# Gate bias of a mixer trunk: seeded into the PSUM banks by ScalarE instead of added by matmuls

## The chip, the cores and the metric

The kernel runs on one core of a Trainium2 chip. The metric is the device time of one execution in microseconds (us). The engines are PE (TensorE), ACT (ScalarE), DVE (VectorE), POOL (GpSimd) and SP (SyncE, which here only issues DMAs).

## The reference

One decoder layer over 256 tokens of width 2048. Four token mixers (differential attention, mLSTM, gated linear attention "GLA", and S5) run on one projection of `h`. Each mixer's output is projected, multiplied by its own sigmoid gate, and summed; an output projection and a SwiGLU FFN follow.

```python
branches = (o_a, o_b, o_c, o_d)
merged = [jax.nn.sigmoid(h @ w_gate[l, i] + b_gate[l, i]) * (branches[i] @ w_branch[l, i])
          for i in range(N_BRANCH)]
mix = (merged[0] + merged[1] + merged[2] + merged[3]) @ w_out[l]
```

Only the term `+ b_gate[l, i]` is touched here: 4 branches times 2048 channels, the same for all 256 tokens.

## The kernel before, in words

Weights come from DRAM as 128x2048 f32 tiles (1 MB, tile `raw`, a ring of 3 buffers, loaded on SP's queue). ACT casts each half of a tile to a high part (`whi`, a CAST at L135), DVE subtracts to get the low part (`wlo`). A product is three matmuls per k step: `xh·wh`, `xh·wl`, `xl·wh` (`mm3t`), in rows `mmt<-whi,hx` and `mmt<-wlo,hx`.

The gate stage works through 16 groups (i, ng): branch i, 512 output channels ng. A group has four weight tiles (kq = 0 to 3), each giving 24 matmuls of 512 columns, 12 for each of two PSUM banks (`mmt`, one bank per 128 tokens, 4 buffers). When the fourth is done, ACT copies both banks into the SBUF tile `sig{i}{ng}` (`COPY sig<-mmt`), and later applies the sigmoid to it in place (`ACTIVATE sig<-sig`). The `sig` tiles come from a pool `f4` of 15 buffers. In order: the gates of branches 0 and 1, branch projections 0 and 1, gates 2, branch 2, gates 3, branch 3.

After each weight tile the mixers, written as generators, are advanced: three steps of a serial chain (attention, then mLSTM, then GLA) and a fraction of a step of S5. A mixer step goes back and forth: PE makes a product or a transpose into PSUM (`mxt`, `bu`, `ys`), ACT or DVE reads it, and PE needs the result again. The tile framework's scheduler then fixes the order in which each engine runs its instructions; each engine runs its own queue strictly in that order.

The bias of a group is added on PE. `gate_bias` prepares once a 128x256 tile `bhl` (high and low parts of all biases) and a selection tile `bsel`; at kq == 0 four matmuls `mmt<-bhl,bsel` of 256 columns open the two banks of the group, and the 96 weight matmuls add to them.

Of the kernel before, what the change touches and what calls it, by code (L numbers as in the profile page):

```python
# [11 lines left out]
F32R = mybir.dt.float32r  # L12
# [7 lines left out]
P = 128  # L20
# [47 lines left out]
def trunk(ctx: ExitStack, tc: tile.TileContext, A: dict, out: bass.AP):  # L68
# [101 lines left out]
    def f4t(name):  # L170
        return f4.tile([P, 4, 256], F32, name=name, tag="f4")
# [33 lines left out]
    for q in range(4):  # L205
        t = f4t(f"xT{q}")
# [78 lines left out]
        while len(hx) <= j:  # L285
            next(chunk_steps)


    bhl = mxc.tile([P, 256], F32R, name="bhl")
    bsel = mxc.tile([P, 32], F32R, name="bsel")  # L290

    def gate_bias():
        t = f4t("braw").rearrange("p a b -> p (a b)")
        ve.memset(t, 0.0)
        for q in range(4):
            sy.dma_start(t[32 * q : 32 * q + 16, 0:256], A["b_gate"][q // 2])
        sy.dma_start(t[:, 512:544], A["bsel"])
        se.copy(bsel, t[:, 512:544])
        se.copy(t[:, 256:512].bitcast(F32R), t[:, 0:256])
        for q in (0, 64):  # L300
            se.copy(bhl[q : q + 32, :], t[q : q + 32, 0:256])
            tt(bhl[q + 32 : q + 64, :], t[q + 32 : q + 64, 0:256], t[q + 32 : q + 64, 256:512], SUB)

    k0 = 0
    for r, kr in enumerate(ROUNDS):
        last = r == len(ROUNDS) - 1
        ahead = 0 if last else 3 * ROUNDS[r + 1]
        rest = GROUPS
        if r == 0:
            lead, rest = GROUPS[:NLEAD], GROUPS[NLEAD:]  # L310
            lb = {g: held[g] if g in held else [mmtile(), mmtile()] for g in lead}
            for ka in range(0, kr, 2):
                kb = min(ka + 2, kr)
                need(kb - 1)
                for g, gname in enumerate(lead):
                    get = weights(A["w_in0"][g][:, ka * 512 : kb * 512])
                    group_mm(lb[gname], get, [(k - ka, k) for k in range(ka, kb)], ka == 0, kb == kr)
            for gname in lead:
                if gname not in held:
                    group_out(gname, lb[gname], True)  # L320
        need(k0 + kr - 1)
        for i, gname in enumerate(rest):
            g = GROUPS.index(gname)
            gets = [weights(A[f"w_in{r}"][g][:, c : min(c + 2048, kr * 512)]) for c in range(0, kr * 512, 2048)]

            def get(off, width):
                return gets[off // 2048](off % 2048, width)

            keep = gname in held
            banks = held[gname] if keep else [mmtile(), mmtile()]  # L330
            group_mm(banks, get, [(k, k0 + k) for k in range(kr)], r == 0 or not keep, True)
            if not keep or last:
                group_out(gname, banks, r == 0 or keep)
            if last:
                take_ada(AW[i])
            for _ in range(ahead * (i + 1) // len(rest) - ahead * i // len(rest)):
                next(chunk_steps)
        get = weights(A[f"w_sm{r}"])
        bank = mmtile()
        for k in range(kr):  # L340
            mm2(bank, get(k * P, P), hx[k0 + k], k == 0, k == kr - 1)
        if r == 0:
            se.copy(small, bank[:, 0:256])
        else:
            tt(small, bank[:, 0:256], small, ADD)
        tt(small, bank[:, 256:512], small, ADD)
        if r == 1:
            gate_bias()
        k0 += kr


# [462 lines left out]
    def gate_unit(i, n):  # L814

        ng, kq = divmod(n, 4)
        get = weights(A["w_gate"][i, ng, kq])
        if kq == 0:
            gate_unit.banks = [mmtile(), mmtile()]
            for bank in gate_unit.banks:  # L820
                c = 4 * i + ng
                for q in range(2):
                    mm(bank[:, q * 256 : q * 256 + 256], bsel[:, q * 16 + c : q * 16 + c + 1].broadcast_to([P, P]),
                       bhl, q == 0, False)
        for tok, bank in enumerate(gate_unit.banks):
            for k in range(4):
                mm3t(bank, get(k * 512, 512), hx[4 * kq + k], tok, False, kq == 3 and k == 3)
        if kq == 3:
            t = f4t(f"sig{i}{ng}")
            sig[i, ng] = t  # L830
            for tok, bank in enumerate(gate_unit.banks):
                se.copy(by_token(t)[:, tok, :], bank)
        if n == NK - 1:
            for q in range(4):
                act(sig[i, q], sig[i, q], AF.Sigmoid)
# [251 lines left out]
def layout(i):  # L1087
# [41 lines left out]
    for r, kr in enumerate(ROUNDS):  # L1129
# [4 lines left out]
        k0 += kr  # L1134
    a["w_gate"] = c_(np.asarray(i["w_gate"], f)[0].reshape(4, 4, 4, P, 4, 512).transpose(0, 4, 1, 3, 2, 5)
                     .reshape(4, 4, 4, P, D))
    a["b_gate"] = c_(np.asarray(i["b_gate"], f).reshape(16, 2, 256).transpose(1, 0, 2))
    bs = np.zeros((P, 32), f)
    bs[:16, :16] = bs[32:48, :16] = bs[64:80, 16:] = bs[96:112, 16:] = np.eye(16, dtype=f)
    a["bsel"] = bs  # L1140
    a["w_branch"] = c_(np.asarray(i["w_branch"], f)[0].reshape(4, 4, P, 4, 512).transpose(0, 3, 2, 1, 4)
                       .reshape(4, 4, P, D))
    a["w_out"] = c_(np.asarray(i["w_out"], f)[0].reshape(4, 4, P, 4, 512).transpose(3, 0, 2, 1, 4)
# [64 lines left out]
```

## Time and profile before

| | us |
|---|---|
| median of 3 runs | 1692.04 (1691.89 to 1694.96) |
| the profiled execution | 1693.66 |
| its span in the trace | 1691.9 |
| PE busy | 1652.8 |
| DVE busy | 1242.0 |
| ACT busy | 874.8 |

The span is what the trace covers of the profiled execution; the remaining 1.8 us lie around it. PE's mean granted clock was 0.993 of full speed. Gate and branch stages lie between about 280 and 840 us.

### The profile page before, as it was taken

The numbers are of one execution on the slowest core, as the hardware profiler recorded it, in microseconds if no ns is written. First come the engines' busy times: TensorE is split into PE (matmuls) and PEld (weight loads), VectorE is DVE, ScalarE is ACT, GpSimd is POOL, SyncE is SP. The second block draws the span as 40 slices with busy tenths as digits, with TensorE's granted clock in tenths as the row PEclk, the third lists the DMA queues.
The fourth block names the chain that finished last, engine by engine and source line by source line (L and its number), as shares of the span: only waits on it lengthen the run. The fifth ranks groups of instructions, "written<-read, shape, count | busy, mean of one in ns | idle before, by whom it ended". The sixth has DMA issues, their size and how long they took to land.

```text
span 1691.9 us, 20679 instructions
## 1 busy us (share of the span) xinstructions
PE 1652.8 (98%) x8000; PEld 1349.1 (80%) x8000; DVE 1242.0 (73%) x1721; ACT 874.8 (52%) x1270; POOL 0.2 (0%) x4
## 2 busy tenths in 40 slices
PE   6999999999999999999999899999999999999997
PEld 4788888777787777777888688888888888888886
DVE  6889999898899998997657766666666555444444
ACT  4544445687675465465445744444444444444342
POOL 0000000000000000000000000000000000000000
PEclk8999999999999999999999899999999999999999
DMA  9887886865556765765566266666665555555553
GB/s 370 358 339 306 317 353 256 298 253 211 195 214 251 294 251 187 263 252 191 207 239 258 100 224 225 245 228 245 227 244 203 192 182 190 211 197 199 189 187 121
DMA packets 61134, 400.69 MB, mean 237 GB/s; under 512 B 6881, under 2 KB 10470, under 8 KB 13676
## 3 DMA queue, kind: packets, MB, share of 16 engines
q1 hardware_dynamic: 60460, 398.33, 63.7%
q8 instruction: 62, 1.02, 0.2%
q10 hardware_dynamic: 576, 1.05, 0.2%
q14 instruction: 36, 0.29, 0.1%
HBM read 397.23 MB, written 2.12 MB: 236 GB/s over the span
## 4 chain that ended last, share of the span: by engine, by line
PE 90%; DVE 5%; DMA 2%; ACT 1%; issue 1%; SPq 0%; DVEq 0%; ACTq 0%
PE mmt L94 83%; PE mxt L94 4%; DVE wlo L73 1%; PE hs L94 1%; DVE raw L81 1%; PE ys L94 1%; PE bu L94 1%; DMA raw<-in_w_in 1%; DMA raw<-in_w_gate 1%; DVE sig L73 0%; DMA vp<-in_vp 0%; DMA hank<-sd 0%; ACT whi L135 0%; DVE zz L781 0%; PE mxt L385 0%
## 5 line engine op out<-in xcount | busy, mean ns | idle before, releaser
L73 DVE TENSOR_TENSOR wlo<-raw,whi 128x1024 fp32r<-128x1024 f32 (+1 forms) x548 | 663.4, 1219 | 368.4 <-ACT whi L135 360.6
L135 ACT CAST whi<-raw 128x1024 fp32r<-128x1024 f32 (+1 forms) x548 | 567.9, 1046 | 528.0 <-PE mmt L94 403.7
L94 PE MATMUL mmt<-whi,hx 128*128 128x512 f32 x1600 | 510.9, 394 | 1.6 <-ACT whi L135 1.6
L94 PE MATMUL mmt<-h,whi 128*128 128x512 f32 x1408 | 498.9, 400 | 0.3 <-DVE h L73 0.3
L94 PE MATMUL mmt<-h,wlo 128*128 128x256 f32 x1408 | 395.8, 281 | 0.0
L94 PEld LDWEIGHTS mmt<-whi,hx 128*128 128x128 f32 x1600 | 299.3, 188 | 72.9 <-issue 9.9
L94 PEld LDWEIGHTS mmt<-h,whi 128*128 128x128 f32 x1408 | 265.1, 188 | 66.7 <-DVE h L73 0.7
L94 PE MATMUL mmt<-wlo,hx 128*128 128x512 f32 x800 | 314.4, 393 | 2.2 <-DVE wlo L73 2.2
L94 PEld LDWEIGHTS mmt<-h,wlo 128*128 128x128 f32 x1408 | 266.5, 189 | 0.0
L81 DVE SCALAR_TENSOR_TENSOR raw<-raw,cb 128x2048 f32<-128x2048 f32 x96 | 219.2, 2285 | 16.1 <-ACT cb L91 9.1
L94 PE MATMUL mmt<-whi,hid 128*128 128x512 f32 x704 | 216.8, 389 | 0.0
L94 PEld LDWEIGHTS mmt<-wlo,hx 128*128 128x128 f32 x800 | 150.3, 188 | 37.4 <-DVE wlo L73 4.0
L94 PEld LDWEIGHTS mmt<-whi,hid 128*128 128x128 f32 x704 | 132.2, 188 | 27.3
L94 PE MATMUL mmt<-wlo,hid 128*128 128x512 f32 x352 | 136.9, 389 | 0.0
L94 PE MATMUL mmt<-whi,os 128*128 128x512 f32 x256 | 82.4, 398 | 0.0
L94 PE MATMUL mmt<-whi,mx 128*128 128x512 f32 x256 | 80.0, 392 | 0.0
L94 PEld LDWEIGHTS mmt<-wlo,hid 128*128 128x128 f32 x352 | 66.1, 188 | 13.8
L91 ACT ACT_TABLE_LOAD x58 | 74.4, 1283 | 1.9 <-PEq L1197 0.7
L94 PEld LDWEIGHTS mmt<-whi,os 128*128 128x128 f32 x256 | 47.8, 188 | 12.5 <-issue 0.8
L94 PEld LDWEIGHTS mmt<-whi,mx 128*128 128x128 f32 x256 | 48.0, 188 | 10.1
L94 PE MATMUL mmt<-wlo,os 128*128 128x512 f32 x128 | 51.0, 401 | 2.0 <-DVE wlo L73 2.0
L94 PE MATMUL mmt<-wlo,mx 128*128 128x512 f32 x128 | 50.4, 393 | 0.0
(280 smaller groups left out, 1131.2 us busy)
## 6 DMA issues: line engine op xcount, KB each, us to landing
raw<-in_ada SPq DMA_DIRECT2D x96, 1024.0 KB, 5.3
raw<-in_ffn_in SPq DMA_DIRECT2D x88, 1024.0 KB, 4.9
raw<-in_w_gate SPq DMA_DIRECT2D x64, 1024.0 KB, 4.8
raw<-in_ffn_out SPq DMA_DIRECT2D x44, 1024.0 KB, 4.8
raw<-in_w_in SPq DMA_DIRECT2D x42, 1024.0 KB, 6.9
raw<-in_w_branch SPq DMA_DIRECT2D x16, 1024.0 KB, 5.4
raw<-in_w_out SPq DMA_DIRECT2D x16, 1024.0 KB, 4.8
xT<-in_xT SPq DMA_DIRECT2D x4, 512.0 KB, 8.4
```

Source lines behind the costliest of these rows:

```text
L73: return ve.tensor_tensor(out=o, in0=a, in1=b, op=op)
L81: return ve.scalar_tensor_tensor(out=o, in0=a, scalar=s, in1=b, op0=op0, op1=op1, accum_out=accum)
L91: return se.activation(out=o, in_=i, func=f, **kw)
L94: return te.matmul(o, lhsT=l, rhs=r, start=start, stop=stop, skip_group_check=True)
L135: se.copy(hi[:, :n], s)
```

## The change

`gate_bias` and its two tiles go, and so do the 64 bias matmuls. At kq == 0 of a group its `sig` tile is now allocated (before: at kq == 3), and one DMA on SP's queue repeats the group's 512 biases over the 128 partitions into the first half of that tile (128x512). ACT copies this row block into each of the two banks (`COPY mmt<-sig`, L807), and the first weight matmul of each bank adds to what stands there. At kq == 3 the banks are drained into the same tile as before. The host passes the biases as 4x4x512.

```diff
@@ -285,22 +285,6 @@
         while len(hx) <= j:
             next(chunk_steps)
 
-
-    bhl = mxc.tile([P, 256], F32R, name="bhl")
-    bsel = mxc.tile([P, 32], F32R, name="bsel")
-
-    def gate_bias():
-        t = f4t("braw").rearrange("p a b -> p (a b)")
-        ve.memset(t, 0.0)
-        for q in range(4):
-            sy.dma_start(t[32 * q : 32 * q + 16, 0:256], A["b_gate"][q // 2])
-        sy.dma_start(t[:, 512:544], A["bsel"])
-        se.copy(bsel, t[:, 512:544])
-        se.copy(t[:, 256:512].bitcast(F32R), t[:, 0:256])
-        for q in (0, 64):
-            se.copy(bhl[q : q + 32, :], t[q : q + 32, 0:256])
-            tt(bhl[q + 32 : q + 64, :], t[q + 32 : q + 64, 0:256], t[q + 32 : q + 64, 256:512], SUB)
-
     k0 = 0
     for r, kr in enumerate(ROUNDS):
         last = r == len(ROUNDS) - 1
@@ -344,8 +328,6 @@
         else:
             tt(small, bank[:, 0:256], small, ADD)
         tt(small, bank[:, 256:512], small, ADD)
-        if r == 1:
-            gate_bias()
         k0 += kr
 
 
@@ -816,18 +798,18 @@
         ng, kq = divmod(n, 4)
         get = weights(A["w_gate"][i, ng, kq])
         if kq == 0:
+            t = f4t(f"sig{i}{ng}")
+            sig[i, ng] = t
+            row = t[:, 0:2, :].rearrange("p a b -> p (a b)")
+            sy.dma_start(row, A["b_gate"][i, ng : ng + 1, :].broadcast_to([P, 512]))
             gate_unit.banks = [mmtile(), mmtile()]
             for bank in gate_unit.banks:
-                c = 4 * i + ng
-                for q in range(2):
-                    mm(bank[:, q * 256 : q * 256 + 256], bsel[:, q * 16 + c : q * 16 + c + 1].broadcast_to([P, P]),
-                       bhl, q == 0, False)
+                se.copy(bank, row)
         for tok, bank in enumerate(gate_unit.banks):
             for k in range(4):
                 mm3t(bank, get(k * 512, 512), hx[4 * kq + k], tok, False, kq == 3 and k == 3)
         if kq == 3:
-            t = f4t(f"sig{i}{ng}")
-            sig[i, ng] = t
+            t = sig[i, ng]
             for tok, bank in enumerate(gate_unit.banks):
                 se.copy(by_token(t)[:, tok, :], bank)
         if n == NK - 1:
@@ -1134,10 +1116,7 @@
         k0 += kr
     a["w_gate"] = c_(np.asarray(i["w_gate"], f)[0].reshape(4, 4, 4, P, 4, 512).transpose(0, 4, 1, 3, 2, 5)
                      .reshape(4, 4, 4, P, D))
-    a["b_gate"] = c_(np.asarray(i["b_gate"], f).reshape(16, 2, 256).transpose(1, 0, 2))
-    bs = np.zeros((P, 32), f)
-    bs[:16, :16] = bs[32:48, :16] = bs[64:80, 16:] = bs[96:112, 16:] = np.eye(16, dtype=f)
-    a["bsel"] = bs
+    a["b_gate"] = c_(np.asarray(i["b_gate"], f).reshape(4, 4, 512))
     a["w_branch"] = c_(np.asarray(i["w_branch"], f)[0].reshape(4, 4, P, 4, 512).transpose(0, 3, 2, 1, 4)
                        .reshape(4, 4, P, D))
     a["w_out"] = c_(np.asarray(i["w_out"], f)[0].reshape(4, 4, P, 4, 512).transpose(3, 0, 2, 1, 4)
```

How the instructions stand on the engines. The scheduler's order changes with it, at three places above all. In these rows `sig_2389` (before) and `sig_2132` (after) are the tile of group (0,0), `sig_2439` that of (0,1), `sig_2717` of (0,2), `sig_3809` of (1,2), `sig_4129` of (1,3).

**Place A**, where PE goes from group (0,0) to group (0,1), while attention is at its softmax (`lg` logits, `pT` transposed probabilities). PE before, the end of group (0,0), the bias, and the first part of group (0,1):

```order
L94 MATMUL mmt<-whi,hx 128x512
L94 MATMUL mmt<-bhl,bsel 128x256 x4
L94 MATMUL mmt<-whi,hx 128x512
L94 MATMUL mmt<-wlo,hx 128x512
L94 MATMUL mmt<-whi,hx 128x512 x2
L94 MATMUL mmt<-wlo,hx 128x512
L94 MATMUL mmt<-whi,hx 128x512 x2
L475 MATMUL mxt<-ident,lg 128x128
L94 MATMUL mmt<-wlo,hx 128x512
L94 MATMUL mmt<-whi,hx 128x512 x2
L94 MATMUL mmt<-wlo,hx 128x512
L94 MATMUL mmt<-whi,hx 128x512 x2
```

A transpose of `lg` stands after five rows of the group, and more gate matmuls follow it before PE comes to the products with `pT`. PE of the changed kernel, from the last matmul of group (0,0) to the first two of group (0,1):

```order
L94 MATMUL mmt<-whi,hx 128x512
L457 MATMUL mxt<-ident,lg 128x128
L94 MATMUL mxt<-da_v,pT 128x128
L457 MATMUL mxt<-ident,lg 128x128 x2
L94 MATMUL mxt<-da_v,pT 128x128 x2
L94 MATMUL mxt<-da_kT,da_qT 128x128
L94 MATMUL mxt<-da_kT,da_qT 128x256
L94 MATMUL mxt<-da_kT,da_qT 128x128
L94 MATMUL mxt<-da_kT,da_qT 128x256
L94 MATMUL mmt<-whi,hx 128x512
L94 MATMUL mmt<-wlo,hx 128x512
```

All of attention's step, three transposes, three products with `pT` and the next block's four `da_kT,da_qT`, now stands between the two groups with no gate matmul among it. ACT of the changed kernel at the same place:

```order
L459 COPY pT<-mxt 128x128
L814 COPY sig_2132<-mmt 128x512
L465 COPY oda<-mxt 128x128
L135 CAST whi<-raw 128x1024
L91 ACTIVATE jk,ssa<-oda 128x128
L459 COPY pT<-mxt 128x256
L91 ACT_TABLE_LOAD
L91 ACTIVATE sig_2132<-sig_2132 128x1024
L465 COPY oda<-mxt 128x128
L91 ACTIVATE jk,ssa<-oda 128x128
L135 CAST whi<-raw 128x1024
L807 COPY mmt<-sig_2439 128x512 x2
```

The seeds of group (0,1), the last row, stand behind the copies of that same attention step, two casts, a table load and a sigmoid.

**Place B**, from group (0,1) to group (0,2), attention's next block and S5. PE before, the bias and what follows it:

```order
L94 MATMUL mmt<-whi,hx 128x512
L94 MATMUL mxt<-da_v,pT 128x128
L475 MATMUL mxt<-ident,lg 128x128 x2
L94 MATMUL mmt<-bhl,bsel 128x256 x4
L94 MATMUL mmt<-whi,hx 128x512
L94 MATMUL mmt<-wlo,hx 128x512
L94 MATMUL mxt<-da_v,pT 128x128 x2
L385 MATMUL mxt<-ident,s_u 128x128 x4
L94 MATMUL mmt<-whi,hx 128x512 x2
L94 MATMUL mxt<-da_kT,da_qT 128x128
L94 MATMUL mxt<-da_kT,da_qT 128x256
L94 MATMUL mxt<-da_kT,da_qT 128x128
```

PE of the changed kernel, from the last matmul of group (0,1) to the first of (0,2):

```order
L94 MATMUL mmt<-whi,hx 128x512
L94 MATMUL mxt<-da_kT,da_qT 128x128 x2
L94 MATMUL mxt<-da_kT,da_qT 128x256 x2
L732 MATMUL bu<-ident,ba 128x128 x2
L94 MATMUL bu<-s_uT,bbT 128x256 x4
L94 MATMUL mmt<-whi,hx 128x512
```

The products `da_kT,da_qT`, which had gate matmuls on both sides, and S5's `bu` now stand in one piece ahead of the group. ACT of the changed kernel, from the drain of group (0,1)'s second bank to the seeds of (0,2):

```order
L814 COPY sig_2439<-mmt 128x512
L135 CAST whi<-raw 128x1024
L91 ACT_TABLE_LOAD
L91 ACTIVATE sig_2439<-sig_2439 128x1024
L733 COPY bbT<-bu 128x256
L91 ACT_TABLE_LOAD
L91 ACTIVATE lg,st<-lg,st 128x128 x2
L91 ACTIVATE lg,st<-lg,st 128x256 x2
L807 COPY mmt<-sig_2717 128x512 x2
```

The four exponentials of the softmax, which read those products, and two table loads have come to stand ahead of the seeds.

**Place D**, from group (1,2) to group (1,3), the end of GLA (`gatt`, `gatx`, `ogl`) and S5. PE before, from the bias into the group:

```order
L94 MATMUL mmt<-bhl,bsel 128x256 x4
L94 MATMUL mmt<-whi,hx 128x512
L94 MATMUL mmt<-wlo,hx 128x512
L94 MATMUL mmt<-whi,hx 128x512 x2
L94 MATMUL mmt<-wlo,hx 128x512
L94 MATMUL mmt<-whi,hx 128x512 x2
L94 MATMUL mmt<-wlo,hx 128x512
L94 MATMUL mmt<-whi,hx 128x512 x2
L94 MATMUL mmt<-wlo,hx 128x512
L94 MATMUL mmt<-whi,hx 128x512 x2
L94 MATMUL mmt<-wlo,hx 128x512
L94 MATMUL mxt<-gqe,gE 128x64 x8
```

GLA's eight products `gqe,gE` come after ten rows of the group's gate matmuls, and the rest of GLA lies between later ones. PE of the changed kernel, the last part of what stands ahead of the group's first matmul (ahead of these rows stand the same eight `gqe,gE`, two `bu` and five `gl_v,gatt`, and before those the last matmul of group (1,2)):

```order
L94 MATMUL mxt<-gl_v,gatx 128x128
L94 MATMUL mxt<-gl_v,gatt 128x128
L94 MATMUL mxt<-gl_v,gatx 128x128
L94 MATMUL mxt<-gl_v,gatt 128x128
L94 MATMUL mxt<-gl_v,gatx 128x128
L94 MATMUL mxt<-gl_v,gatt 128x128
L94 MATMUL mxt<-gl_v,gatx 128x128
L94 MATMUL ys<-xc,cd 32x256 x2
L378 MATMUL mxt<-ident,ogl 128x128
L94 MATMUL bu<-s_uT,bbT 128x256 x2
L378 MATMUL mxt<-ident,ogl 128x128 x3
L94 MATMUL mmt<-whi,hx 128x512
```

GLA's last step runs in one piece between the two groups. ACT of the changed kernel there:

```order
L91 ACTIVATE jk,gss<-mxt 128x128 x4
L91 ACTIVATE fx<-fx 128x256
L91 ACT_TABLE_LOAD
L91 ACTIVATE gss<-gss,epst 128x4
L91 ACTIVATE jk,gss<-mxt 128x128 x4
L91 ACT_TABLE_LOAD
L91 ACTIVATE cs<-fx,hp 128x256
L91 ACT_TABLE_LOAD
L91 ACTIVATE gss<-gss,epst 128x4
L91 ACT_TABLE_LOAD
L91 ACTIVATE sig_3809<-sig_3809 128x1024
L807 COPY mmt<-sig_4129 128x512 x2
```

The seeds of group (1,3) stand behind eight squares `jk`, four table loads and the sigmoid of group (1,2); ahead of these rows stand that group's second drain copy, a cast, a fifth table load and one `cs`.

A fourth place, **C**, from group (0,2) to (0,3), is alike: PE runs eight `ident,ml_k` transposes, four `ys`, two `bu` and two `small,ident` ahead of the group; on ACT the second drain copy of (0,2), two `ml_kT` copies, eight `mlqc` and `mlkc` scalings and a cast stand ahead of the seeds. At the 12 other groups the seeds stand on ACT about a weight tile or more ahead of the group's first matmul.

## Rows read from the trace of the kernel before

**Rows 1.** Page, part 1: busy time of the engines, share of the span, instructions.

```profile
PE 1652.8 (98%) x8000; PEld 1349.1 (80%) x8000; DVE 1242.0 (73%) x1721; ACT 874.8 (52%) x1270; POOL 0.2 (0%) x4
```

**Rows 2.** Page, part 4: the chain that ended last, by engine.

```profile
PE 90%; DVE 5%; DMA 2%; ACT 1%; issue 1%; SPq 0%; DVEq 0%; ACTq 0%
```

**Rows 3.** Windows 280 to 800 us, sums: length, then busy time per engine.

```profile
sum 520.00, PE 513.37 PEld 395.46 DVE 466.35 ACT 326.18 POOL 0.00; mean PE 39.49 PEld 30.42 DVE 35.87 ACT 25.09 POOL 0.00
```

**Rows 4.** Tile bhl: bias matmuls; ns min/median/max, first and last start.

```profile
L94 PE MATMUL mmt<-bhl,bsel x64: 276/279/385, 284.2 to 788.9; 128*128 128x256 f32 x64
```

**Rows 5.** Timeline of PE, first group: start, us, instruction.

```profile
284.22 0.62 PE L94 MATMUL mmt<-bhl,bsel 128*128 128x256 f32 x4
284.68 0.40 PE L94 MATMUL mmt<-whi,hx 128*128 128x512 f32 x1
```

**Rows 6.** Timeline of PE around the second group, attention's matmuls.

```profile
306.63 0.93 PE L94 MATMUL mxt<-da_kT,da_qT 64*128 64x128 f32 x8
...
317.71 0.38 PE L475 MATMUL mxt<-ident,lg 128*128 128x128 f32 x2
...
318.92 0.71 PE L94 MATMUL mxt<-da_v,pT 128*128 128x128 f32 x4
```

**Rows 7.** Timeline of DVE, last step ahead of attention's transposes.

```profile
314.38 0.74 DVE L81 SCALAR_TENSOR_TENSOR lg<-lg,st 128x128 f32<-128x128 f32 x2
```

**Rows 8.** Timeline of ACT around the second group.

```profile
309.61 0.40 ACT L91 ACTIVATE lg<-lg,st 128x128 f32<-128x128 f32 x1 [1.60 <-DVE st L462]
...
311.38 0.57 ACT L832 COPY sig<-mmt 128x512 f32<-128x512 f32 x1
...
313.76 1.05 ACT L135 CAST whi<-raw 128x1024 fp32r<-128x1024 f32 x1
314.82 1.28 ACT L91 ACT_TABLE_LOAD   x1
316.12 1.06 ACT L91 ACTIVATE sig<-sig 128x1024 f32<-128x1024 f32 x1
...
318.20 0.31 ACT L91 ACTIVATE jk<-oda 128x128 f32<-128x128 f32 x1
...
318.51 0.35 ACT L477 COPY pT<-mxt 128x256 f32<-128x256 f32 x1
```

**Rows 9.** Timeline of ACT around the fourth group, mLSTM's copies and scalings.

```profile
371.82 0.59 ACT L832 COPY sig<-mmt 128x512 f32<-128x512 f32 x1 [0.31 <-PE mmt L94]
...
376.60 0.92 ACT L91 ACTIVATE mlkc<-ml_kT,vp 128x256 f32<-128x256 f32 x2
```

**Rows 10.** Timeline of ACT around group (1,3), GLA's end.

```profile
508.91 0.28 ACT L91 ACTIVATE jk<-mxt 128x128 f32<-128x128 f32 x1
...
509.93 1.06 ACT L135 CAST whi<-raw 128x1024 fp32r<-128x1024 f32 x1
...
516.34 0.42 ACT L91 ACTIVATE cs<-fx 128x256 f32<-128x256 f32 x1
```

**Rows 11.** Timeline of PE around group (1,3), GLA and S5.

```profile
504.47 1.11 PE L94 MATMUL mxt<-gqe,gE 64*128 64x64 f32 x16
...
510.51 0.39 PE L94 MATMUL mxt<-gl_v,gatt 128*128 128x128 f32 x2
510.74 0.39 PE L94 MATMUL mxt<-gl_v,gatx 128*128 128x128 f32 x2
511.05 1.05 PE L94 MATMUL ys<-xc,cd 128*32 128x256 f32 x4
```

**Rows 12.** Timeline of PE at the largest wait; a wait and its releaser in brackets.

```profile
941.51 2.00 PE L988 MATMUL mxt<-ident,mixt 128*128 128x128 f32 x8 [7.24 <-DVE mixt L77]
```

**Rows 13.** Windows of 2 us there: busy per engine, then PE's granted clock.

```profile
938.00:940.00 2.00, 0.00 (x0) 0.00 (x0) 2.00 (x6) 2.00 (x8) 0.00 (x0) 0.50 0.00 0
...
946.00:948.00 2.00, 2.00 (x11) 1.77 (x10) 1.44 (x6) 1.76 (x6) 0.00 (x0) 0.74 0.00 0
```

**Rows 14.** Page, part 6: loads of the gate weights, KB, us to landing.

```profile
raw<-in_w_gate SPq DMA_DIRECT2D x64, 1024.0 KB, 4.8
```

## The prediction

> **What bounds the kernel now.** I read the page's busy times first. PE, which does all products, is busy 98% of the span [rows 1]; the reader should see that little is left for anything but removing PE work. The chain that ended last agrees: 90% of it is PE [rows 2]. The stage of the change lies between 280 and 800 us, so I then added PE's busy time there in windows of 40 us: 513.37 of 520 us [rows 3], that is 6.6 us idle. Inside the stage PE is the bound, and ACT and DVE (326 and 466 us of 520) are not, on average. So two questions decide: how much PE time goes, and whether PE has to wait for something new.
>
> **What the change removes.** There are 64 bias matmuls, four per group, 276 to 385 ns each by their records [rows 4]. Records of PE overlap, so the price is read from the starts: the four of the first group begin at 284.22, the next weight matmul at 284.68 [rows 5], hence 0.46 us a group and 16 x 0.46 = **7.4 us**. The preparation of the bias (two casts, two subtractions, five small DMAs) lies long before on engines that PE isn't shown waiting for; I count 0 for it.
>
> **What it adds and that costs nothing by itself.** 32 ACT copies of 128x512 between SBUF and PSUM. The trace has the copy in the other direction, 0.57 us [rows 8]; 32 of them are 18 us of ACT, which has 194 us free in the stage [rows 3]. A copy into PSUM isn't in the trace; bounds are that 0.57 and the 1.05 of a cast of twice the columns [rows 8], and I take 0.57. Without the free time ahead of the matmuls it would cost 16 x 0.57 = 9 us. 16 DMAs of 256 KB written; a weight tile of 1024 KB lands in 4.8 us [rows 14], so a quarter of its bytes should take no longer. What covers them is the time between issue and the group's first matmul. If the cover is gone PE waits up to 4.8 us per group; I come to this below.
>
> **What it moves: the waits.** The bias matmuls needed nothing that was new. Now the first matmul of a group waits for the first seed copy, and that copy waits its turn on ACT's queue. Where ACT's queue holds, ahead of the seed, work that reads the mixer's products, the scheduler has put those products on PE ahead of the group too. Then PE runs a mixer step end to end, with its back and forth to ACT, and has no gate matmuls to fill the gaps. This is so at places A to D. The price of each is ACT's work from the last matmul of the old group to the seed, less what PE itself does in that time. (On PE an fp32 product leaves two records, a transpose one: x4 of pT is two products.)
>
> Place A. ACT after the first transposes: one drain copy 0.57, two casts of 1.06 (313.76 to the table load at 314.82) 2.12, table load and start of the sigmoid 1.30 (314.82 to 316.12), sigmoid 1.06, four small copies at most 0.35 each, I take 1.2 for the four, two squares with their read-out 0.31 each (318.20 to 318.51) 0.62, and the seed like a drain copy 0.57, all from [rows 8]: 7.4 us. PE in that time: three transposes (0.38 for two) 0.57, three products with pT (0.71 for two) 1.07, four logits products 0.93 [rows 6]: 2.6. Idle 4.8. In front of it the transposes wait for DVE: from the end of the logits products, 306.63 + 0.93 = 307.56 [rows 6], to the end of DVE's last step, 314.38 + 0.74 = 315.12 [rows 7], it took 7.56 us, and only one weight tile now lies between on PE, 24 x 0.23 = 5.5 us (the step of 512-column matmuls: 0.46 us for the four bias matmuls is two such steps). That is 2.1 more. A = **6.9 us**.
>
> Place B. ACT: drain 0.57, cast 1.06, table and sigmoid 1.30 + 1.06, the bbT copy 0.35, a second table load 1.28, four exponentials 1.77 (309.61 to 311.38), seed 0.57 [rows 8]: 8.0. PE: four logits products 0.93, two transposes 0.38 [rows 6], four bu. One of these has 256 fp32 columns like ys, of which two take 1.05 [rows 11], so 2.1. Together 3.4. B = **4.5 us**.
>
> Place C. The same ACT sequence stands in the trace of before, where gate matmuls ran beside it: from the drain at 371.82 to the end of the last scaling at 376.60 + 0.92 it took 5.7 us [rows 9], with the seed 6.3. PE: eight transposes at 0.19 each 1.5 [rows 6], eight products of 256 columns at 0.53 each 4.2 [rows 11]: 5.7. About 0.6; ys also waits for DVE, and if those eight products ran only behind ACT's sequence it would be 4.2 more. C = **1 us**, bounds 0 and 5.
>
> Place D. ACT until the first square: drain 0.57, cast 1.06, table load 1.30, cs 0.42 [rows 8, 10] = 3.4. Then twice four squares, 1.02 for four (508.91 to 509.93), fx, cs and two gss at most 0.42 each, I take 1.4 [rows 10], four table loads of 1.28, sigmoid 1.06, seed 0.57 [rows 8]: 10.2. Together 13.6. PE: eight gqe products 1.11, twelve gl_v products at 0.22 (510.51 to 510.74 is a row of one product) 2.7, four bu and two ys at 0.53 3.2 [rows 11], four ogl transposes 0.8 [rows 6]: 7.7. D = **5.9 us**.
>
> Together 6.9 + 4.5 + 1 + 5.9 = 18.3 us. At the other 12 groups ACT has a weight tile's time (5.5 us) in hand, and I count 0.
>
> **The clock.** After PE's one long wait, 7.24 us before 941.51 [rows 12], the granted clock stood at 0.50, which of its two levels is 1.2 GHz, and it was 0.74 on average at 946 to 948, so back at the upper one near 947 [rows 13]. PE worked at half speed for 5.5 us, which lost about 2.7. The Trainium skill ("TensorE: Matmul & The Clock Gate", "Part 1: The HAM clock gate") says that the clock is throttled by default and activity releases it; the trace agrees, with 0.50 after that idle stretch. The gaps at A to D are broken up by short mixer products, so whether the clock falls in them can't be read; 0 to 4 x 2.7 = 10.8 us, and I take one, 2.7.
>
> **Sum.** -7.4 + 18.3 + 2.7 = +13.6 us. On the profiled execution's 1693.66 that is 1707.3; that execution stands 1.6 above the median of the runs, and on the median it is 1705.6. I forecast 1706 us, 0.8% slower. About 0.2%, 3.4 us, is what a measurement here can tell from no change.
>
> A page speaks on the table loads, eight of which stand in my chains (A one, B two, D five). The rows show a load at 314.82 of 1.28 us and the sigmoid at 316.12, nothing between [rows 8]. The Trainium skill ("ScalarE: Activation LUTs", "What ACT_TABLE_LOAD costs") adds a drain of some 1.38 us to each. By that, as an estimate, eight loads would cost 11 us more; the trace shows no such drain.
>
> **Rivals.**
> - *The waits don't happen, only the gain stays.* If ACT came to the seeds while PE still worked on mixer steps, as it does at 12 groups, the time is 1692.0 - 7.4 = 1684.6. It needs ACT to be more than 4 us ahead at A, B and D. Against it: ACT's drain at 371.82 and the later rows follow PE's last matmul directly, and the seeds stand behind that drain in the queue. Chance 0.06.
> - *The waits happen and are given back.* While PE waits, ACT, DVE and the loads run ahead up to their buffers, and the 6.6 us that PE idled in the stage [rows 3] go. With A and D at their low ends (front of A hidden, C zero): 15.2 - 6.6 - 7.4 = +1.2, 1693.2, within the bound. Chance 0.07.
> - *The clock falls in each of the four gaps*: 8.1 us more than my sum, 1714. Chance 0.2. For it speaks that ACT's chains at A and D take 7 and 14 us; against it that PE works about half of that time.
> - *The bias rows come late.* Their DMAs stand on SP behind loads of weight tiles that wait for a ring buffer. If SP reaches them only when PE has used up the tile before, each of the four groups waits part of 4.8 us [rows 14], say 2, or up to 4.8 x 4 = 19 us more: 1713 to 1725. It also holds up the weight loads behind it where the f4 pool has no free buffer. Chance 0.15.
> - *A drain behind each table load*, the page's rule: 11 us more, 1716. No row bears it out; chance 0.02.
>
> My own case has the remaining 0.50. Its range is 1700 to 1712. The whole range must reach from near the give-back case to the late rows: 1697 to 1721. Below lie the faster case and most of the give-back case, above the worst of the late rows. Chances: faster 0.07, same 0.07, slower 0.86.
>
> **What would show it.** Right: PE idle of some 5 us at A, B and D in the windows of the changed kernel (near 313, 342 and 500 us), ended by ACT's seed copy or by ACT and DVE work of the mixers; 16 x 0.46 us less PE work; bias rows landed before ACT reaches the seeds. Wrong: PE's busy time in 280 to 800 as full as before, or PE's waits spread evenly over all 16 groups (then the seeds or rows are late as such, not because of the mixers), or a granted clock well below 1 for long.

## The result and the profile after

The changed kernel takes 1712.22 us in the median (1701.14 to 1712.67, 8 runs) against 1693.61 for the kernel before on the same chips: a ratio of 1.0102, 95% interval 1.0082 to 1.0122. It is slower by 1.0%. The forecast was 1706, slower by 0.8%, range 1697 to 1721. (Of the runs of e3 below one, at 2057.84 us and a mean granted clock of 0.748, is in the median but not in the ratio.)

The page of the changed kernel, busy times (answers to [rows 1]):

```profile
PE 1655.2 (97%) x7936; PEld 1352.2 (79%) x7936; DVE 1242.8 (73%) x1718; ACT 899.2 (53%) x1304; POOL 0.2 (0%) x4
```

PE is busy 2.4 us longer than before although 64 of its matmuls are gone, and of the span of 1710.4 us it stands idle 55.2, where it was 39.1 of 1691.9. Windows of 40 us of the changed kernel (length, busy time of PE, weight loads, DVE, ACT, POOL with counts, PE's granted clock, DMA share, GB/s):

```profile
280.00:320.00 40.00, 35.29 (x160) 26.94 (x158) 32.00 (x78) 26.94 (x46) 0.00 (x0) 0.96 0.77 296
320.00:360.00 40.00, 33.87 (x152) 25.31 (x152) 33.62 (x69) 32.17 (x70) 0.00 (x0) 0.89 0.63 226
360.00:400.00 40.00, 35.40 (x156) 27.06 (x157) 35.67 (x67) 27.68 (x49) 0.00 (x0) 0.88 0.61 223
400.00:440.00 40.00, 39.74 (x186) 32.31 (x184) 34.86 (x54) 33.67 (x46) 0.00 (x0) 0.97 0.64 229
440.00:480.00 40.00, 38.63 (x188) 29.88 (x187) 30.48 (x57) 29.52 (x45) 0.00 (x0) 1.00 0.50 186
...
520.00:560.00 40.00, 35.48 (x151) 26.92 (x150) 34.07 (x60) 27.23 (x51) 0.00 (x0) 0.87 0.63 230
```

Before, PE stood idle 2.0 us in 280 to 560, at clock 1.00 throughout; now it is idle 21.6 us there, and the clock is below 1 in the four windows with more than 4 us of idle time and in 400 to 440, the one after C. For 280 to 800 the sum row, which answers to [rows 3]:

```profile
sum 520.00, PE 496.76 PEld 382.57 DVE 458.64 ACT 340.50 POOL 0.00; mean PE 38.21 PEld 29.43 DVE 35.28 ACT 26.19 POOL 0.00
```

23.2 us idle in place of 6.6. For the seeds themselves PE waited only 5.6 us in 280 to 930 (total, times, longest):

```profile
PE mmt L94 <- ACT mmt L807: 5.6, 4, 4.3
```

Nearly all its new waits lie at five places, to be seen in PE's timeline (start, us, instruction, idle before it and what ended that). First group (0,0) and place A:

```profile
309.59 0.50 PE L94 MATMUL mmt<-wlo,hx 128*128 128x512 f32 x1 [2.71 <-DVE wlo L73]
...
316.93 0.49 PE L94 MATMUL mxt<-da_v,pT 128*128 128x128 f32 x2 [0.35 <-ACT pT L459]
...
319.27 0.71 PE L94 MATMUL mxt<-da_v,pT 128*128 128x128 f32 x4 [1.64 <-ACT pT L459]
319.92 1.28 PE L94 MATMUL mxt<-da_kT,da_qT 64*128 64x128 f32 x4
321.80 1.65 PE L94 MATMUL mxt<-da_kT,da_qT 64*128 64x128 f32 x4 [0.60 <-ACT oda L465]
323.65 0.80 PE L94 MATMUL mmt<-whi,hx 128*128 128x512 f32 x1 [0.21 <-ACT mmt L807]
```

Place B, then C, then D:

```profile
356.57 1.13 PE L94 MATMUL bu<-s_uT,bbT 32*128 32x256 f32 x4 [3.02 <-ACT bbT L733]
360.08 2.04 PE L94 MATMUL bu<-s_uT,bbT 32*128 32x256 f32 x4 [2.39 <-DVE st L446]
```

```profile
396.92 0.80 PE L94 MATMUL mmt<-whi,hx 128*128 128x512 f32 x1 [4.33 <-ACT mmt L807]
```

```profile
528.78 0.47 PE L378 MATMUL mxt<-ident,ogl 128*128 128x128 f32 x1 [3.20 <-DVE ogl L81]
530.22 2.04 PE L94 MATMUL bu<-s_uT,bbT 32*128 32x256 f32 x4 [0.97 <-DVE pq L73]
...
533.27 0.79 PE L94 MATMUL mmt<-whi,hx 128*128 128x512 f32 x1 [0.18 <-ACT mmt L807]
```

Four of the five are the places A to D, where the group's first matmul comes after a mixer step that ran alone. Only at C does PE wait long for the seed; at A and D the seed adds 0.2 us, and at B PE goes from the last `bu` to the group without a wait. The fourth wait for a seed, 0.86 us at 608.20, is at group (2,0). The fifth place, 2.71 us at 309.59, was not foreseen: DVE now does attention's first step ahead of a split. Two-us windows at A show the clock:

```profile
322.00:324.00 2.00, 1.79 (x5) 1.07 (x6) 1.18 (x6) 2.00 (x5) 0.00 (x0) 0.50 1.03 434
324.00:326.00 2.00, 2.00 (x6) 1.52 (x6) 2.00 (x6) 1.97 (x5) 0.00 (x0) 0.50 0.97 401
326.00:328.00 2.00, 2.00 (x8) 1.60 (x7) 1.89 (x7) 1.98 (x7) 0.00 (x0) 0.71 0.27 115
```

PE waited 1.64 us before 319.27 and 0.60 before 321.80; the clock stood at 0.50 from 322 to 326, when PE had its gate matmuls again, and came back near 327.

Why the seeds are late is seen one queue further up. SP's timeline (issue of the bias rows of groups (0,1), (0,2), (0,3), and of six rows, (1,3) the first, three of them with the load just ahead of it):

```profile
314.11 0.33 SPq L119 DMA_DIRECT2D raw<-in_w_gate  x1
314.49 0.42 SPq L804 DMA_DIRECT2D sig<-in_b_gate  x1
...
353.32 0.33 SPq L119 DMA_DIRECT2D raw<-in_w_gate  x1
353.70 0.42 SPq L804 DMA_DIRECT2D sig<-in_b_gate  x1
...
390.13 0.38 SPq L804 DMA_DIRECT2D sig<-in_b_gate  x1
...
525.77 0.33 SPq L119 DMA_DIRECT2D raw<-in_ada  x1
526.15 6.53 SPq L804 DMA_DIRECT2D sig<-in_b_gate  x6
```

and ACT's seeds of the same groups:

```profile
323.02 1.10 ACT L807 COPY mmt<-sig 128x512 f32<-128x512 f32 x2
```

```profile
360.17 1.11 ACT L807 COPY mmt<-sig 128x512 f32<-128x512 f32 x2 [0.48 <-DMA sig<-in_b_gate]
```

```profile
396.27 1.11 ACT L807 COPY mmt<-sig 128x512 f32<-128x512 f32 x2 [0.54 <-DMA sig<-in_b_gate]
```

```profile
532.64 1.09 ACT L807 COPY mmt<-sig 128x512 f32<-128x512 f32 x2
```

At B and C the last thing that the seed waited for was its row, for 0.48 and 0.54 us; at A and D ACT's own work ended last. At D the row was issued only 6.5 us ahead of the seed. A row of 256 KB took 4.0 to 6.8 us to land (the changed kernel's line of row loads):

```profile
DMA to landing us min/median/max: 4.0/5.4/6.8
```

The row loads of A, B and C wait, in SP's order, on a semaphore of PE:

```
L804 DMA sig_2439<-in_b_gate 128x512 [waits PE_49]
L804 DMA sig_2717<-in_b_gate 128x512 [waits PE_49]
L804 DMA sig_2996<-in_b_gate 128x512 [waits DMAHW4_49,PE_49]
```

So the row lies in the `sig` tile, that tile takes a buffer of pool `f4`, and the buffer is free only when PE has read a mixer's older tile out of it. This trace doesn't show that this came last: at A and B SP issued the row 0.05 us after a weight load that had itself waited for DVE, at C behind another such load and at D behind an `ada` load, so the wait on PE was over when SP came to the row. For the row of B other runs show it: SP stood waiting for PE 6.1 us in e3, until 351.10, and 7.8 us in f6, until 351.83.

### The profile page after: what moved, and what is told of

Its sections match the earlier page's. It is cut to its first block, busy times and chain, and to the rows that moved or that the text cites. A ratio compares the mean times of both kernels' runs of the same rounds, so it can differ in the third digit from the quotient of the medians.

```text
span 1710.4 us, 20619 instructions
## 1 busy us (share of the span) xinstructions
PE 1655.2 (97%) x7936; PEld 1352.2 (79%) x7936; DVE 1242.8 (73%) x1718; ACT 899.2 (53%) x1304; POOL 0.2 (0%) x4
## 3 DMA queue, kind: packets, MB, share of 16 engines
q10 hardware_dynamic: 576, 1.05, 0.2%
## 4 chain that ended last, share of the span: by engine, by line
PE 90%; DVE 5%; ACT 2%; DMA 2%; issue 1%; SPq 0%; DVEq 0%
PE mmt L94 83%; PE mxt L94 3%; DVE raw L81 1%; PE hs L94 1%; DVE wlo L73 1%; DMA raw<-in_ada 1%; PE ys L94 1%; PE bu L94 1%; ACT whi L135 0%; ACT L91 0%; DVE sig L73 0%; DMA sig<-in_b_gate 0%; DMA raw<-in_w_gate 0%; DVE pc L73 0%; PE mxt L367 0%
## 5 line engine op out<-in xcount | busy, mean ns | idle before, releaser
L94 PE MATMUL mmt<-whi,hx 128*128 128x512 f32 x1600 | 516.5, 399 | 7.2 <-ACT mmt L807 5.6
L94 PEld LDWEIGHTS mmt<-whi,hx 128*128 128x128 f32 x1600 | 304.2, 191 | 81.8 <-issue 9.3
L94 PE MATMUL mmt<-wlo,hx 128*128 128x512 f32 x800 | 318.1, 398 | 3.8 <-DVE wlo L73 3.8
```

What stands on the lines that cost most here:

```text
L94: return te.matmul(o, lhsT=l, rhs=r, start=start, stop=stop, skip_group_check=True)
```

## The experiments

Each was timed against the kernel before on the same chip. Theory of the prediction: the seeds wait on ACT's queue behind mixer work. After the trace above a second one stood beside it, the slot theory: the row's buffer is what is late, and the whole order at A to D follows from that. Rivals: the copies and row loads cost by themselves; the DMA queue. The kernel before took 1693.50 us in the median beside e2, e3, e4 and e11, 1694.50 beside f1 to f4, 1694.76 beside e6 and f5, and 1692.89 beside f6 and f7.

| run | median us | ratio to before, 95% |
|---|---|---|
| changed kernel | 1712.22 | 1.0102 [1.0082, 1.0122] |
| e2, no bias matmuls | 1700.09 | 1.0032 [1.0013, 1.0050] |
| e4, seeds from a resident tile | 1696.63 | 1.0012 [1.0002, 1.0023] |
| e3, rows and no seeds | 1700.37 | 1.0014 [0.9997, 1.0031] |
| e11, rows in buffers of their own | 1700.70 | 1.0040 [1.0019, 1.0061] |
| e6, seeds on DVE | 1733.75 | 1.0223 [1.0202, 1.0245] |
| f1, before, ada moved | 1688.39 | 0.9960 [0.9947, 0.9973] |
| f4, no bias matmuls, ada moved | 1687.84 | 0.9962 [0.9949, 0.9974] |
| f2, own buffers, ada moved | 1688.62 | 0.9966 [0.9954, 0.9979] |
| f7, one own buffer, ada moved | 1690.58 | 0.9987 [0.9966, 1.0009] |
| f6, sig tile two tiles earlier, ada moved | 1699.14 | 1.0040 [1.0015, 1.0065] |
| f5, bias added by GpSimd, ada moved | 1710.68 | 1.0090 [1.0070, 1.0110] |
| f3, changed kernel, ada moved | 1712.43 | 1.0098 [1.0082, 1.0114] |

**e2: the matmuls taken out, nothing put in.** The bias is left out.

```diff
             gate_unit.banks = [mmtile(), mmtile()]
-            for bank in gate_unit.banks:
-                c = 4 * i + ng
-                for q in range(2):
-                    mm(bank[:, q * 256 : q * 256 + 256], bsel[:, q * 16 + c : q * 16 + c + 1].broadcast_to([P, P]),
-                       bhl, q == 0, False)
...
-                mm3t(bank, get(k * 512, 512), hx[4 * kq + k], tok, False, kq == 3 and k == 3)
+                mm3t(bank, get(k * 512, 512), hx[4 * kq + k], tok, kq == 0 and k == 0, kq == 3 and k == 3)
```

> The kernel before without its 64 bias matmuls (the gates' bias is left out, the banks are opened by the first weight matmul). All theories: only the 7.4 us of the matmuls go, about 1686 us, and PE's order keeps mixer work and gate matmuls interleaved. If it is slower than 1690, freeing PE time is worth less than its sum.

It got slower, 1700.09. PE's order stayed interleaved. The page, beside [rows 1], and three windows:

```profile
PE 1650.9 (97%) x7936; PEld 1345.0 (79%) x7936; DVE 1241.6 (73%) x1721; ACT 879.6 (52%) x1275; POOL 0.2 (0%) x4
```

```profile
400.00:440.00 40.00, 37.54 (x191) 29.67 (x190) 34.01 (x59) 29.30 (x44) 0.00 (x0) 1.00 0.61 227
...
560.00:600.00 40.00, 34.69 (x130) 27.30 (x130) 35.65 (x47) 16.35 (x21) 0.00 (x0) 0.87 0.74 278
...
680.00:720.00 40.00, 37.35 (x152) 28.29 (x151) 35.63 (x45) 14.39 (x16) 0.00 (x0) 0.96 0.65 239
```

PE is idle 46.3 of 1697.2 us in place of 39.1 of 1691.9, so 7.2 us more, and its busy time fell by only 1.9 us instead of 7.4. The most idle time, 5.3 us, lies in 560 to 600, in the branch projections, but 3.7 us were there before as well; what came new is above all 2.7 us in 680 to 720 and 2.5 in 400 to 440, where before there was none. PE's timeline in 560 to 600 (a third wait of the same length follows at 710.90), and then that of the kernel before:

```profile
564.28 0.50 PE L94 MATMUL mmt<-wlo,os 128*128 128x512 f32 x1 [2.65 <-DVE wlo L73]
...
579.95 0.79 PE L94 MATMUL mmt<-wlo,os 128*128 128x512 f32 x1 [2.65 <-DVE wlo L73]
```

```profile
570.00 0.50 PE L94 MATMUL mmt<-wlo,os 128*128 128x512 f32 x1 [2.03 <-DVE wlo L73]
...
584.12 0.50 PE L94 MATMUL mmt<-wlo,hx 128*128 128x512 f32 x1 [1.72 <-DVE wlo L73]
```

PE now comes earlier to splits that DVE finishes no earlier. In e2 the clock was 0.87 on average in that window, where before, with the shorter waits, it stayed at 1.00:

```profile
560.00:600.00 40.00, 36.26 (x158) 28.48 (x157) 39.18 (x51) 18.09 (x22) 0.00 (x0) 1.00 0.76 287
```

So the saved PE time was lost in waits, and slower matmuls took more.

**e4, e3: seeds without row loads, and row loads without seeds.** e4 copies from the resident tile `cb` (a wrong bias); e3 leaves the seeds, and so the bias, out.

```diff
-            row = t[:, 0:2, :].rearrange("p a b -> p (a b)")
-            sy.dma_start(row, A["b_gate"][i, ng : ng + 1, :].broadcast_to([P, 512]))
+            row = cb[:, 0:512]
```
```diff
-            for bank in gate_unit.banks:
-                se.copy(bank, row)
...
-                mm3t(bank, get(k * 512, 512), hx[4 * kq + k], tok, False, kq == 3 and k == 3)
+                mm3t(bank, get(k * 512, 512), hx[4 * kq + k], tok, kq == 0 and k == 0, kq == 3 and k == 3)
```

> The changed kernel, but the 32 ACT seeds copy from a tile that is resident from the start, and no bias rows are loaded (the gates get a wrong bias). Theory of the slot (the seed is late because its row lies in the sig tile, whose buffer of pool f4 is free only when a mixer is done with it): the four places A to D go, 1686 to 1690 us. Theory of ACT's queue (the seed is late because ACT has other work ahead of it): seeds stay late, 1700 to 1712. Rival, price of the copies themselves (32 x 0.57 us): 1700 to 1710, with waits spread over the groups.

> The changed kernel with the row loads into the early allocated sig tiles, but without the 32 seeds (the bias is left out). Slot theory: no PE instruction waits for the rows, 1686 to 1690 us. Rival of the queue of DMAs (row loads that wait for a buffer hold up weight loads behind them on SP): 1695 to 1712. ACT's queue: 1686.

1696.63 and 1700.37: neither half makes the changed kernel's 1712. In both, the pieces A to D are gone from PE's order. In e3 SP issues the row of (0,1) at 313.56, as late as in the changed kernel, and behind a weight load as there; a late row makes no such place where no seed needs it. 32 seeds that need no row cost nothing beside e2, so the price of the copies is out as a cause, and so is ACT's queue by itself. Both missed the 1686 to 1690 as e2 did: e4 waits 2.65 us at 571 and 3.47 at 588 for `wlo`, e3 2.65 at 577 and 2.34 at 593, and 4.2 in three waits at 457 to 463 for `whi` and `wlo`.

**e11: the whole change, rows in two buffers of their own.**

```diff
-NF4 = 15
+NF4 = 14
...
+    browp = mixers.enter_context(tc.tile_pool(name="browp", bufs=2))
...
-            t = f4t(f"sig{i}{ng}")
-            sig[i, ng] = t
-            row = t[:, 0:2, :].rearrange("p a b -> p (a b)")
+            row = browp.tile([P, 512], F32, name="brow", tag="brow")
...
         if kq == 3:
-            t = sig[i, ng]
+            t = f4t(f"sig{i}{ng}")
+            sig[i, ng] = t
```

> The whole change, but the bias row goes into one of two buffers of its own instead of the first half of the sig tile, which is allocated at the drain again (pool f4 gives up one of its 15 buffers for the space). Slot theory: rows come early, seeds too, A to D go, 1686 to 1690 us, faster than both kernels. ACT's queue: 1700 to 1712. Price of copies and rows themselves: about 1712.

1700.70: A to D gone, 11.5 us faster than the changed kernel, but not at 1688. The row of group (0,1) was issued at 295.99 instead of 314.49, and its seeds no longer stand behind attention. SP's and ACT's timelines:

```profile
295.99 0.49 SPq L803 DMA_DIRECT2D brow<-in_b_gate  x1
```

```profile
310.28 1.09 ACT L806 COPY mmt<-brow 128x512 f32<-128x512 f32 x2
```

What is left is mainly the loss of e2, idle in 560 to 600 and the clock with it, and the fifth place, which is thus no part of what A to D cost:

```profile
560.00:600.00 40.00, 33.14 (x126) 25.69 (x127) 38.20 (x48) 19.04 (x25) 0.00 (x0) 0.91 0.75 279
```

```profile
308.80 0.79 PE L94 MATMUL mmt<-wlo,hx 128*128 128x512 f32 x1 [2.71 <-DVE wlo L73]
```

**f1, f4, f2, f3: the second limit relieved.** The longest waits of e2 lie in the branch projections, where each unit of branches 0 to 2 also takes an `ada` tile, 2.29 us of DVE. These were moved into the gate units of branches 2 and 3. (They are 12, not the 16 of the expectation: the list of `ada` tiles is used up before branch 3.) Up to the first branch projection PE's order stays that of the kernel each is made from.

```diff
-AR = (0.7, 0.5, 0.3, 0.3)
-AB = 1
+AR = (0.7, 0.5, 0.7, 0.7)
+AB = 0
```

> The kernel before, with the 16 ada tiles (2.29 us of DVE each) that stood in the branch projections moved into the gate units of branches 2 and 3. Theory of the second limit (in the branch projections DVE's splits are late however fast PE comes, so PE time saved ahead of them turns into waits there): the 3.7 us of waits for DVE near 570 to 585 us go, about 1690 us. Rival (gain lost elsewhere): within 1692 to 1695.

> The kernel before without the 64 bias matmuls (the gates' bias is left out), with the same move of ada tiles. Second limit: now the 7.4 us count, 1682 to 1686 us, 6 to 8 below the kernel before with that move, and the 2.65 us waits for wlo in the branch projections go. Rival: as far above the kernel before with the move as it was without it, about 1697 to 1700.

> The whole change with rows in two buffers of their own, with the same move of ada tiles. Second limit: 1684 to 1688 us, faster than before by 0.3 to 0.5%. Rival, price of the seeds and rows themselves: 1692 to 1700.

> The changed kernel as it is, with the same move of ada tiles. The four places A to D stand in the order as before, and no waits are left in its branch projections to relieve: 1706 to 1712 us, some 22 above the kernel with rows of their own, which would be the full price of the four places. Rival, that A to D are not what costs: 1690 to 1700.

f1 1688.39, f4 1687.84, f2 1688.62, f3 1712.43. By the ratios the move is worth 0.4% to the kernel before, 0.7% to e2 and e11, and nothing to the changed kernel. f3 less f2 is 23.8 us: the price of A to D with nothing to give back later. But f4 is faster than f1 by only 0.55 us, which the intervals don't tell from none, against the second limit's forecast of 6 to 8 us. The sum over 280 to 800 of f1, and a window and the sum of f4:

```profile
sum 520.00, PE 518.45 PEld 400.22 DVE 463.67 ACT 325.88 POOL 0.00; mean PE 39.88 PEld 30.79 DVE 35.67 ACT 25.07 POOL 0.00
```

```profile
400.00:440.00 40.00, 37.55 (x170) 28.84 (x167) 30.60 (x53) 27.02 (x42) 0.00 (x0) 0.91 0.58 214
...
sum 520.00, PE 512.82 PEld 393.70 DVE 463.87 ACT 329.68 POOL 0.00; mean PE 39.45 PEld 30.28 DVE 35.68 ACT 25.36 POOL 0.00
```

The waits of the branch projections are gone in both (PE is busy the full 40 us in 560 to 600), but f4 idles 5.6 us more than f1 elsewhere, the most for `whi` near 401 and 419, for `wlo` near 403 and 773 and for ACT's `pT` near 342, and the clock is 0.91 in 400 to 440 and 0.96 in 760 to 800. Over the whole span f4's PE is busy 8.1 us less than f1's and idle 6.3 us more. So in these two profiles the limit is not one place: PE time saved became waits along the stage, mostly for the splits of ACT and DVE. Each profile is one execution, the slowest of its kernel's (1693.44 and 1691.72); f1's own has a clock of 0.91 in 440 to 480, after a wait of 1.53 us at 460, which runs at 1688 need not have had.

**e6: the seeds on DVE.**

```diff
-                se.copy(bank, row)
+                ve.tensor_copy(out=bank, in_=row)
```

> The changed kernel with the 32 seed copies on DVE instead of ACT, rows in the sig tiles as changed. In PE's order places A, C and D stand as in the changed kernel, B is smaller. Slot theory (the row can be loaded only when a mixer has let go of the buffer, whoever copies it): 1703 to 1713 us, the gaps at A and D of 8 to 10 us still there. Theory of ACT's queue: the seeds no longer stand behind ACT's work, 1697 to 1701 like the kernel with rows of their own.

1733.75, outside both ranges, so this run decides for neither theory. The copies now stand in the queue of DVE, the engine that PE waits for in e2:

```profile
L807 DVE COPY mmt<-sig 128x512 f32<-128x512 f32 x32 | 21.1, 685 | 5.5 <-DMA sig<-in_b_gate 3.5 <-ACT sig L814 2.0
```

```profile
PE mmt L94 <- DVE mmt L807: 18.8, 5, 6.0
```

Taking the copies off ACT didn't free PE from waiting for them, which is against ACT's queue as the whole cause; how much of the 21 us over the changed kernel is the fuller DVE queue and how much the row is not told apart.

**f6, f7: only the moment, and only one buffer** (both with ada moved). f6 keeps the sig tile and 15 buffers, and allocates and loads two weight tiles earlier; f7 is f2 with `bufs=1`.

```diff
...
+        u = 16 * i + n + 2
+        if u == 2:
+            load_row(0)
+        if u % 4 == 0 and 0 < u < 64:
+            load_row(u // 4)
...
```

> The changed kernel with only the moment changed at which a group's sig tile is allocated and its row load issued: two weight tiles earlier (pool f4 keeps 15 buffers), ada tiles moved as before. In PE's order A and D are gone, of B and C a part is left. Slot theory: between the kernel with rows of its own and the changed one, 1690 to 1700 us, idle left only at B and C. If the place in the sig tile is no cause: about 1712.

> As the kernel with rows in two buffers of their own and ada tiles moved, but one row buffer instead of two. Slot theory: a row then waits only for the seeds of the group before, which lie a group's time back, so 1685 to 1690 us, like two buffers. If the rows' landing is what is short: slower than with two, 1692 or more.

f6 1699.14, f7 1690.58 (its interval overlaps f2's). f6 lies between, as the slot theory has it, but its idle time is not only at B and C; in attention's next block PE waits for copies (the profile is of an execution of 1692.42 us, below the median):

```profile
346.00 0.66 PE L367 MATMUL mxt<-ident,s_u 128*128 128x128 f32 x4 [2.09 <-ACT oda L465]
```

**f5: no seeds at all, GpSimd adds the row to the drained tile** (ada moved).

```diff
...
                 se.copy(by_token(t)[:, tok, :], bank)
+                nc.gpsimd.tensor_tensor(out=by_token(t)[:, tok, :], in0=by_token(t)[:, tok, :], in1=gate_unit.row, op=ADD)
...
```

> No seeds and no bias matmuls: the row, in one of two buffers of its own, is added by GpSimd to the drained sig tile; ada tiles moved as in the runs before. If the seeds still cost waits in the kernel with rows of their own, this is faster than it: 1684 to 1687 us. If PE time saved is lost to DVE's and ACT's splits whatever is done with the bias, 1687 to 1690. If GpSimd's adds slow DVE down, 1690 and above.

1710.68, the third case. GpSimd's adds, and one of DVE's groups in that kernel:

```profile
L813 POOL TENSOR_TENSOR sig<-sig,brow 128x512 f32<-128x512 f32 x32 | 63.8, 1999 | 767.8 <-ACT sig L812 765.1 <-DMA raw<-in_w_gate 2.6
```

```profile
L81 DVE SCALAR_TENSOR_TENSOR fx<-iota,sp,fx 128x256 f32<-128x256 f32 x32 | 18.4, 574 | 0.2
```

The same DVE group has a mean of 480 ns in f2, and DVE's busy time is 1261.0 us against 1240.7. The group's median stays at 478 ns; the longest took 1514. So a few operations took about 1 us longer, three of them in this group, each while one of GpSimd's adds ran. DVE is slower with GpSimd in use, and DVE is an engine that PE waits for; how much of the 22 us over f2 comes from this alone no run shows.

No version that adds the bias is faster than f1, which is the kernel before with ada tiles moved and without the change.

## Why the prediction came out right, point by point

- **"hence 0.46 us a group and 16 x 0.46 = 7.4 us".** The matmuls are that long, but the step from PE time to run time failed. In f4 the 7.4 us gave 0.55 us (1688.39 to 1687.84), in e2 a loss of 6.6. The runs show in its place: saved PE time becomes waits, mostly for the splits of ACT and DVE, and the clock falls after some of them. Of ACT and DVE (466 of 520 us on DVE) the prediction had said that they "are not, on average" the bound; with DVE busy 90% of the stage, that average left little for PE to gain.
- **The waits, 18.3 us.** Place by place, forecast and idle time in the timeline above: A 6.9 and 2.8 (0.35 + 1.64 + 0.60 + 0.21); B 4.5 and 5.4; C 1 and 4.3; D 5.9 and 4.4; and 2.7 in group (0,0) that were not foreseen. Together 19.6, near the sum by errors that cancel, which is luck. A came out smaller because the front of 2.1 did not come, and because the four logits products took 2.9 us (1.28 + 1.65), partly at the half clock, where 0.93 was counted. C came out larger: its row held the seed up by only 0.54 us, but ACT, which the forecast let start with the drain copy, first did a table load and a `cs`, so the drain began 1.5 us after the transposes (388.55), and PE's own work there took 4.0 us (388.55 to 391.56 + 1.03) instead of 5.7:

```profile
388.45 1.28 ACT L91 ACT_TABLE_LOAD   x1
...
390.06 0.57 ACT L814 COPY sig<-mmt 128x512 f32<-128x512 f32 x1
```

- **"0 to 4 x 2.7 = 10.8 us, and I take one, 2.7".** This term was mis-sized. The clock fell at all four places and at the fifth. PE's busy time rose by 2.4 us although 7.4 us of matmuls went, so what PE did took 9.8 us longer, and the half clock is the one thing that the windows show for it. Taken from the windows above, (1 - clock) x busy, it would be 0.04 x 35.29 + 0.11 x 33.87 + 0.12 x 35.40 + 0.03 x 39.74 + 0.13 x 35.48 = 15.2 us; that is an estimate from above, since much of PE's idle time fell into the half clock. The rival that had the clock fall in each gap, 1714, with a chance of 0.2, is the one that came nearest.
- **The reason of the order.** "that copy waits its turn on ACT's queue" is what A and D show in the run. What puts the mixer's step ahead of the group is the seed's need of a row in a `sig` tile: e4, without a row, e3, without a seed, and e11, with a row elsewhere, have the same ACT and SP and no such places. That the scheduler does so because the tile's buffer comes free late fits f6, where loading two tiles earlier removed part of the loss, and at B the waits of SP for PE in e3 and f6; at A, C and D it is argued and not shown. The rival of late rows, "behind loads of weight tiles", had the queue right: at A and B the row came out behind such a load. But e3 has that too and no places. The sign "bias rows landed before ACT reaches the seeds" failed at B and C.
- **Given back later.** Where the kernel before waited 2.03 and 1.72 us for splits, the changed kernel waits 0.19, and 0.86 for a seed at 608.20:

```profile
596.58 0.50 PE L94 MATMUL mmt<-wlo,os 128*128 128x512 f32 x1 [0.19 <-DVE wlo L73]
```

  DVE catches up while PE stands at A to D. That part of the rival was right. The move of the `ada` tiles takes 6.1 us off the kernel before and nothing off the changed one, and so 23.8 us (f3 less f2) show as 18.6 between before and after.
- **The sum.** Between the two profiled executions, 18.5 us apart, PE idles 16.1 us more and is busy 2.4 more, the -7.4 and 9.8 above. So the forecast of -7.4 + 18.3 + 2.7 had the waits, all told, 2 us too large and the clock 7 us too small. That it came within the range is in part luck: the 7.4 us counted as gained are worth nearly nothing by themselves (f4), and about as much, which the sum left out, was given back at other waits.
- **The drain behind each table load**: at 353.91 the changed kernel loads a table for 1.28 us and the sigmoid starts at 355.20, 0.01 us after its end. The Trainium skill ("ScalarE: Activation LUTs", "What ACT_TABLE_LOAD costs") adds some 1.38 us; no load here shows it.

## What to carry to other kernels

An initial value that PE must wait for binds PE to the buffer that the value is loaded into. Before moving work from PE to a copy, look up which pool the copy's source lies in and who reads that pool's older tiles last; a buffer of its own, loaded earlier, undid the four places here, though it made nothing faster than leaving the bias on PE (f2 1688.62, f1 1688.39). And where a second engine is 90% busy in a stage, as DVE was here, time saved on the first may be worth only what the second leaves: take the work out altogether, as in e2, and time that, before building its replacement.

## What the runs showed of the hardware that was not expected

- A load of 256 KB that repeats one row over 128 partitions landed in 5.4 us in the median, no sooner than a weight tile of 1024 KB, 4.9 us in the same kernel. The prediction had taken it to land no later than the tile.
- Idle PE time of a few us, cut up by short products, was followed by a granted clock of 0.50 at each of the places A to D, and PE then had some 3 to 5.5 us of gate matmuls at half speed (512 columns every 0.43 us in place of 0.23). The length of the single wait didn't decide it: in f4 it came after waits of 1.05, 0.76 and 0.64 us at 401 to 419, and in the kernel before waits of 2.03 and 1.72 us passed without it. Executions of one program differed by several us with it: f2's took 1687.24 to 1688.62 us at a mean clock of 0.992 and 1696.35 at 0.987.
- GpSimd's add of 128x512 took 2.0 us on average (1.28 to 4.12). Four of the 32 `fx` operations of DVE with two SBUF inputs met such an add, and three of them took 1.5 us instead of 0.48; but the one-input `fx<-fx` also rose to 1.26 us in two of three cases, and of 21 `wlo` splits with two SBUF inputs that met an add 19 kept their 1.2 us. The multiplication `sig<-mmt,sig`, with one input from PSUM, stayed at 685 ns, but none of its 32 met an add, so it shows nothing. The Trainium skill ("GPSIMD Engine Reference", "8. Key points") says that GpSimd shares its SBUF interfaces with VectorE and contends with instructions in a 2-port mode or with two SBUF inputs; the `fx` rows agree, most of the splits don't show it.
